# Which pairs of up tiles of an MLP pass take seven quarter products, and a weight split no longer ordered behind evacuations

## The chip, the cores and the metric

The kernel runs on one core of a Trainium2 chip. The metric is the device time of one execution in microseconds (us), as the median of several runs; lower is better. The engines are TensorE (PE; its weight loads are PEld), VectorE (DVE), ScalarE (ACT), GpSimd (POOL) and SyncE (SP, which here only issues DMA transfers). Each engine works through its own instructions strictly in order.

## The reference

Two layers of a decoder trunk in float32, for one sequence of 512 tokens, with D = 1024 and an MLP width of 4096:

```
h = rms_norm(x, ln_mix[l])
x = x + hybrid_mixer(h, ...)        # four token mixers fed by one projection h @ w_in,
                                    # gated sums of their outputs, @ w_out
h = rms_norm(x, ln_mlp[l])
x = x + jnp.square(jax.nn.relu(h @ w_up[l])) @ w_down[l]
```

## The kernel before

**Products.** A float32 product is made of three matmuls, `mm3` (L271): both operands are split into a rounded high part and a rest, and high x high, high x rest and rest x high are added up in PSUM. Weights come from one DRAM array, `wall`, in the order of `plan`. `next_w` (L246) issues a load into one of two `raw` buffers on SP (L255); `split_w` (L258) makes `whi`, a cast on ACT, and then `wlo`, a subtraction on DVE, in one of three buffers each. Nearly all compute instructions are issued through a helper, so that they carry the line L143: tiles are told apart by name.

**Order.** Each engine's order is fixed when the program is built. A scheduler places instructions by priority; `HP()` marks the urgent ones (splits, and the operations that free PSUM). A `NoSync` dependency, as in L264, only tells the scheduler which of two stands first.

**The mixer's first products.** `tok_proj` makes the token-major groups G1, G2 and G3. G2 has 336 columns, four row blocks in four PSUM tiles (`psm`, shown as `tk`). Each is evacuated by two ACT activations, into `sm` and `qe`. `at["hold"]` holds the last of these eight; the next `split_w`, which is that of the first chunk of G3, is ordered behind it. Ahead of that, `rstd` (L348) makes the token scales `rs` on POOL, writes them to DRAM (`rs_dram`, L361) and reads them back across partitions as `rb`, both on POOL's DMA queue. `rsh` is half of `rs`.

**The MLP** (`mlp`, L392) works in four passes of eight up tiles. A pass is four pairs t = 0 to 3, and then a down stage. A normal pair takes two weight chunks of 512 KB through `next_w`, each with 24 matmuls of 512 columns. A pair whose t is in `SEVEN[p]` takes `up_seven` (L420): seven quarter products in place of eight, named A11, S1, S2, S4, S3, A22, A12, of 12 matmuls of 256 columns each. Its four weight quarters (256 KB each, L429) and their sums lie in four `cr` buffers R[0] to R[3]; there are six `cr` buffers in all, and the down stages use them too:

```
B11, S1w, S2w, B22 = R[0][:, lo], R[0][:, up], R[1][:, lo], R[1][:, up]
S3w, all4, B21, B12 = R[2][:, lo], R[2][:, up], R[3][:, lo], R[3][:, up]
sums = {0: ((S1w, B11, B12),), 1: ((S2w, S1w, B22),), 2: ((S3w, B12, B22), (all4, S2w, B21)), 3: ()}
```

The sums are DVE additions (`cr<-cr`), and R[0] to R[3] are split in turn, four splits per pair; R[0] serves A11 and S1, R[1] serves S2 and S4. Before form S3 may add to its PSUM bank, DVE makes U2 = C - U from it (L466, shown as `U<-up,U`). The results are squared in F, cast into `ah` on ACT, and DVE makes the differences `Fs` and the rests `al` (L505 to L511).

The down stage has seven forms too (L639 to L731). Its first is A11, whose PSUM banks (shown as `q`) are those of the fourth pair's tiles, freed by the ReLU that writes F from them (L502). From the second pass on, each result `co` is added into `sum_dram` by an accumulating DMA of POOL's queue (`keep`, L566); so the last of these of one pass run while the up tiles of the next begin. In the last pass `old` (L522) and `xq` (L518) load what the results are joined with.

Of the kernel before, what the change touches and what calls it, by code (L numbers as in the profile page):

```python
# [16 lines left out]
AF = mybir.ActivationFunctionType  # L17
ALU = mybir.AluOpType
# [16 lines left out]
G1K = ((1, 1, 2, 2, 2), (2, 2, 2, 2))  # L35
KORD = ((0, 1, 2, 3, 4, 5, 6, 7), (4, 5, 6, 7, 0, 1, 2, 3))
PASSES = (8, 8, 8, 8)
SEVEN = ((2, 3), (1, 3), (1, 3), (1, 2))
CRB = 6
BIG = 1e30  # L40

# [12 lines left out]
def chunk_plan(l):  # L54
# [30 lines left out]
    for p, nt in enumerate(PASSES):  # L85

        half = nt // 2 * P
        for t in range(0, half, P):
            parts = 2 if t // P in SEVEN[p] else 1
            for i in range(parts):  # L90
# [76 lines left out]
def ins_of(r):  # L167
    return getattr(r, "ins", r)


def trunk(tc, x_in, wall, consts, lps, sgus, out):
    nc = tc.nc
    at = dict(mm=None, side=False, first=None, hold=None)
    V, S, G, T_ = (Paced(tc, e, at) for e in (nc.vector, nc.scalar, nc.gpsimd, nc.tensor))
    HP = lambda off=URGENT: tc.high_priority(offset=off)
    plan = [ch for l in range(NL) for ch in chunk_plan(l)]
    with ExitStack() as es:
# [68 lines left out]
        def next_w(raw=None):  # L246
            kk, n = chunk_shape(plan[pos[0]])
            pos[0] += 1
            L = kk * n
            if raw is None:  # L250
                raw = wpool.tile([P, WCH], F32, name="raw", tag="raw", bufs=WB[0])
            src = wall[off[0]:off[0] + P * L].rearrange("(p l) -> p l", l=L)
            off[0] += P * L
            with HP():
                nc.sync.dma_start(raw[:, :L], src)  # L255
            return split_w(raw, L, n, V.tensor_copy if pos[0] == 1 else S.copy)

        def split_w(raw, L, n, copy=S.copy):  # L258
            hi = wpool.tile([P, WCH], F32R, name="whi", tag="whi", bufs=WB[1])
            lo = wpool.tile([P, WCH], F32R, name="wlo", tag="wlo", bufs=WB[1])  # L260
            with HP():
                c = copy(hi[:, :L], raw[:, :L])
                if at["hold"] is not None:
                    tc.add_manual_dep(ins_of(c), ins_of(at["hold"]).name, V._dep, reason="order")  # L264
                    at["hold"] = None
                r = V.tensor_sub(lo[:, :L], raw[:, :L], hi[:, :L].bitcast(F32))
            at["first"] = r if pos[0] == 1 else None
            return (hi[:, :L].rearrange("p (k n) -> p k n", n=n),
                    lo[:, :L].rearrange("p (k n) -> p k n", n=n))
# [17 lines left out]
        side = []  # L287
# [60 lines left out]
        def rstd(acc, l, late=2):  # L348

            rs, t4 = small["rs"], small["t4"]  # L350
            rb = hpool.tile([P, T], F32, name="rb", tag="rb")

            def gen():
                for _ in range(late):
                    yield
                pa = mmtile("pa", "ms")
                token_sums(pa, acc)
                with HP():
                    V.tensor_scalar(t4, pa[:, 0:4], EPS, None, ALU.add)
                    rpow(rs, t4)  # L360
                G.dma_start(rs_dram[l].rearrange("c p -> p c"), rs)  # L361
                G.dma_start(rb, rs_dram[l].rearrange("c p -> (c p)").partition_broadcast(P))

            side.append(gen())
            return rs, rb
# [26 lines left out]
        def mlp(l, hh, hl, r2, gain, fp, sh, sl):  # L392
# [10 lines left out]
            with tc.tile_pool(name="ap", bufs=1) as ap:  # L403
# [16 lines left out]
                def up_seven(F):  # L420
# [22 lines left out]
                    def form(f, o, i, n, first=True):  # L443
                        if ws[i] is None:
                            for o_, a_, b_ in sums[i]:
                                with HP():
                                    V.tensor_add(o_, a_, b_)
                            ws[i] = split_w(R[i], 512 if i == 3 else 1024, P)
                        w_h, w_l = ws[i]
                        for k in range(4):  # L450
                            bh, bl = moving(f, k)
                            mm3(o, w_h[:, 4 * n + k], w_l[:, 4 * n + k], bh, bl, first and k == 0, k == 3, not first)
                        tick()
# [30 lines left out]
                for p, nt in enumerate(PASSES):  # L484
                    nk = nt // 2
                    ah, al = [], []
                    for t in range(nk):
# [4 lines left out]
                        if t == 1:  # L492
                            early = at["mm"]
                        if t in SEVEN[p]:
                            up_seven(F)
                        for i in range(0 if t in SEVEN[p] else 2):
                            w_h, w_l = next_w()
# [55 lines left out]
                    def use(f, bank, raw, k, first=False):  # L553
                        w_h, w_l = split_w(raw, 1024, 512)
                        for b in range(2):
                            form(f, bank, b, w_h, w_l, k, first)
                        tick()
# [195 lines left out]
        for l in range(NL):  # L753
            with ExitStack() as em:
                x = mixer(tc, em, locals())
            hh, hl = htiles()
            r2 = rstd2(norm(x, lp("ln_mlp"), hh, hl))
            fs = ExitStack()
            fp = fs.enter_context(tc.tile_pool(name="fp", bufs=1))
            forms = quarter_forms(fp, x, lp("ln_mlp"))  # L760
            xs[0].close()
            if l < NL - 1:
                lpt = cpool.tile([P, NLP], F32, name="lp", tag="lp")
                nc.scalar.dma_start(lpt, lps[l + 1])
            nxt, acc = mlp(l, hh, hl, r2, lp("ln_mix"), fp, *forms)
            fs.close()
            if nxt:
                hh, hl = nxt
                rs, rb = rstd(acc, l + 1, 8)
# [3 lines left out]
def mixer(tc, em, env):  # L773
# [9 lines left out]
    def et(name):  # L783
        return yp.tile([P, T], F32, name=name, tag="e", bufs=8)
# [9 lines left out]
    def tt(shape, name, bufs=1, tag=None):  # L794

        p_ = ts if int(np.prod(shape[1:])) % T else tp
        return p_.tile(shape, F32, name=name, tag=tag or name, bufs=bufs)

    if l > 0:
        rs, rb = env["rs"], env["rb"]  # L800
# [14 lines left out]
    def tok_proj(n, kk, chunks, tags, before=None, order=KORD[0], behind=None):  # L815
        pts = {c: mmtile("tk", tags[i]) for i, c in enumerate(chunks)}
        kks = kk if isinstance(kk, tuple) else (kk,) * (KD // kk)
        for k0, kk in zip(np.cumsum((0,) + kks), kks):
            w_h, w_l = next_w(before(k0) if before else None)
            if behind:  # L820
                behind(k0)
            assert not env["at"]["fold"] or order[k0] > 3
            if kk == 1:

                h, first, whole = order[k0], k0 == 0, k0 == KD - 1
                for a, w in ((hh, w_h), (hh, w_l), (hl, w_h)):
                    for c in chunks:
                        env["at"]["mm"] = T_.matmul(pts[c][:, :n], a[h][:, blk(c)], w[:, 0],
                                                    start=first and a is hh and w is w_h, stop=whole and a is hl)
                continue  # L830
            for c in chunks:
                for k in range(kk):
                    mm3(pts[c][:, :n], hh[order[k0 + k]][:, blk(c)], hl[order[k0 + k]][:, blk(c)], w_h[:, k], w_l[:, k],
                        k0 + k == 0, k0 + k == KD - 1)
                if c % 2 == 1:
                    tick()
        return pts
# [49 lines left out]
    else:  # L887
# [28 lines left out]
        rs, rb = rstd(acc[0], 0)  # L916
# [11 lines left out]
    psm = tok_proj(336, 2, range(4), ["mm", "ms", "ms", "ms"])  # L928
    sm = tt([P, 320], "sm").rearrange("p (c w) -> p c w", c=4)
    qe = [et("qe0"), et("qe1")]  # L930
    for c in range(4):
        with HP():
            S.activation(sm[:, c], psm[c][:, 0:80], AF.Identity, scale=rs[:, c:c + 1])
            env["at"]["hold"] = S.activation(qe[c // 2][:, (c % 2) * 256:(c % 2) * 256 + 256], psm[c][:, 80:336],
                                             AF.Identity, scale=rs[:, c:c + 1])
    rsh = tt([P, 4], "rsh")
    V.tensor_scalar(rsh, rs, 0.5, None, ALU.mult)

    def table(n):
        t = et("tab")  # L940
# [403 lines left out]
    for c in range(4):  # L1344
        with HP():
            S.activation(ke[c // 2][:, (c % 2) * 256:(c % 2) * 256 + 256], kvp[c][:, 0:256], AF.Identity,
                         scale=rs[:, c:c + 1])
# [38 lines left out]
    for c in range(4):  # L1386
        with HP():
            S.activation(v2[c // 2][:, (c % 2) * 256:(c % 2) * 256 + 256], pav[c][:, :256], AF.Identity,
                         scale=rs[:, c:c + 1])
    vs = tt([P, 4], "vs")  # L1390
    for c2 in range(2):
        t = et("gv")
        gelu2(v2[c2], t)
        for j in range(2):
            s_ = slice(j * 256, j * 256 + 256)
            c = c2 * 2 + j
# [202 lines left out]
```

## Time and profile before

| | |
|---|---|
| median of 3 runs | 1603.76 us (1603.54 to 1604.75) |
| the profiled execution | 1603.06 us, span of the instructions 1601.3 us |
| PE busy | 1576.8 us, 98% of the span, 8163 matmuls |
| DVE busy | 1238.7 us, 77%, 2127 instructions |
| ACT busy | 756.9 us, 47%, 1168 instructions |
| POOL busy | 144.0 us, 9%, 187 instructions |
| granted TensorE clock | 0.998 over the span |
| DMA | 218.22 MB, mean 136 GB/s |

Busy shares are averages over stages with different limits. The span less PE's busy time, 24.5 us, is all the time in which PE had nothing to run; a stretch in which the granted clock is low counts as busy.

### The profile page before, as it was taken

How to read it: one execution, taken by the hardware profiler on the slowest of the kernel's cores; microseconds unless marked ns; L12 is line 12 of the kernel's file. 1: busy time of each engine (PE TensorE's matmuls, PEld its weight loads, DVE VectorE, ACT ScalarE, POOL GpSimd, SP SyncE). 2: the span in 40 equal slices, each digit the busy share in tenths (PEclk: the TensorE clock that was granted, in tenths of full speed). 3: DMA queues.
4: the chain of work that ended last, by engine and by line, in shares of the span. 5: the costliest groups of instructions: out<-in, count | busy, mean ns of one | idle time of the engine just before them, and what ended most of it. 6: DMA issues, size and time to landing. Idle time of an engine off the chain costs nothing.

```text
span 1601.3 us, 21951 instructions
## 1 busy us (share of the span) xinstructions
PE 1576.8 (98%) x8163; PEld 1322.8 (83%) x8163; DVE 1238.7 (77%) x2127; ACT 756.9 (47%) x1168; POOL 144.0 (9%) x187
## 2 busy tenths in 40 slices
PE   9999999999999999998999999999999999999998
PEld 7888888878888888887888888887888888888887
DVE  6899997645579787867978999975555887867678
ACT  5554224423357474645545433254233674746452
POOL 1322000000001011111013120000000010011110
PEclk9999999999999999999999999999999999999999
DMA  7533322332356466667445232223223465576682
GB/s 179 146 98 110 104 85 99 114 104 95 101 175 165 158 184 158 184 156 221 137 112 155 83 116 96 89 93 135 99 88 111 158 169 176 162 165 171 158 260 83
DMA packets 78411, 218.22 MB, mean 136 GB/s; under 512 B 8896, under 2 KB 16256, under 8 KB 78304
## 3 DMA queue, kind: packets, MB, share of 16 engines
q1 hardware_dynamic: 61360, 175.54, 33.7%
q0 software_dynamic: 16080, 40.27, 13.0%
q8 instruction: 64, 1.05, 0.3%
q10 hardware_dynamic: 864, 1.01, 0.2%
q14 instruction: 43, 0.35, 0.1%
HBM read 192.10 MB, written 21.01 MB: 133 GB/s over the span
## 4 chain that ended last, share of the span: by engine, by line
PE 73%; DVE 13%; issue 5%; ACT 4%; DMA 4%; POOL 0%; SPq 0%; DVEq 0%; ACTq 0%; POOLq 0%
PE g L143 18%; PE up L143 15%; PE tk L143 8%; PE r L143 6%; PE fm L143 6%; PE wo L143 5%; PE q L143 5%; PE p L143 5%; DVE wlo L143 4%; ACT whi L143 2%; DVE sco L143 2%; DMA cr<-in_wall_dram 2%; DMA raw<-in_wall_dram 1%; DVE Fs L143 1%; DVE cr L143 1%
## 5 line engine op out<-in xcount | busy, mean ns | idle before, releaser
L143 ACT CAST whi<-raw 128x1024 fp32r<-128x1024 f32 (+3 forms) x204 | 224.3, 1101 | 199.8 <-DMA raw<-in_wall_dram 64.6
L143 DVE TENSOR_TENSOR wlo<-raw,whi 128x1024 fp32r<-128x1024 f32 (+3 forms) x205 | 262.8, 1283 | 38.5 <-ACT whi L143 37.4
L143 PE MATMUL g<-hh,whi 128*128 128x512 f32 x512 | 200.6, 392 | 0.0
L143 PE MATMUL g<-hh,wlo 128*128 128x512 f32 x512 | 199.5, 390 | 0.0
L143 PE MATMUL g<-hl,whi 128*128 128x512 f32 x512 | 199.3, 389 | 0.0
L143 DVE TENSOR_TENSOR wlo<-cr,whi 128x1024 fp32r<-128x1024 f32 (+1 forms) x144 | 166.6, 1161 | 39.8 <-ACT whi L143 39.5
L143 ACT CAST whi<-cr 128x1024 fp32r<-128x1024 f32 (+1 forms) x144 | 144.3, 1004 | 110.6 <-PE up L143 45.1
L143 PE MATMUL up<-hh,whi 128*128 128x512 f32 (+1 forms) x448 | 155.5, 347 | 0.0
L143 PE MATMUL up<-hh,wlo 128*128 128x512 f32 (+1 forms) x448 | 154.8, 346 | 0.3 <-DVE wlo L143 0.3
L143 PE MATMUL up<-hl,whi 128*128 128x512 f32 (+1 forms) x448 | 154.9, 346 | 0.0
L143 ACT ACTIVATE gs<-gs 128x512 f32<-128x512 f32 x64 | 40.6, 634 | 199.1 <-DVE gs L143 198.9
L143 PEld LDWEIGHTS g<-hh,wlo 128*128 128x128 f32 x512 | 96.1, 188 | 20.3
L143 PEld LDWEIGHTS g<-hh,whi 128*128 128x128 f32 x512 | 96.1, 188 | 19.6
L143 PEld LDWEIGHTS g<-hl,whi 128*128 128x128 f32 x512 | 96.2, 188 | 19.4
L143 PE MATMUL tk<-whi,hh 128*128 128x512 f32 (+2 forms) x304 | 106.9, 358 | 3.9 <-ACT whi L143 3.9
L143 DVE TENSOR_TENSOR cr<-cr 128x512 f32<-128x512 f32 (+1 forms) x80 | 61.7, 793 | 60.4 <-DMA cr<-in_wall_dram 60.1
L143 PE MATMUL tk<-wlo,hh 128*128 128x512 f32 (+2 forms) x304 | 107.3, 355 | 0.2
L143 PE MATMUL tk<-whi,hl 128*128 128x512 f32 (+2 forms) x304 | 106.4, 353 | 0.0
L143 PE MATMUL q<-whi,ah 128*128 128x512 f32 (+1 forms) x260 | 100.9, 392 | 4.2 <-ACT F L143 4.2
L143 DVE TENSOR_TENSOR gs<-g,rb 128x512 f32<-128x512 f32 x64 | 44.1, 689 | 78.7 <-PE g L143 78.6
L143 PE MATMUL q<-whi,al 128*128 128x512 f32 (+1 forms) x260 | 99.8, 389 | 0.0
L143 PE MATMUL q<-wlo,ah 128*128 128x512 f32 (+1 forms) x260 | 99.6, 387 | 0.0
(308 smaller groups left out, 3638.8 us busy)
## 6 DMA issues: line engine op xcount, KB each, us to landing
raw<-in_wall_dram SPq DMA_DIRECT2D x131, 512.0 KB, 4.1
raw<-in_wall_dram SPq DMA_DIRECT2D x64, 640.0 KB, 3.9
cr<-in_wall_dram POOLq DMA_DIRECT2D x48, 512.0 KB, 6.7
cr<-in_wall_dram SPq DMA_DIRECT2D x64, 256.0 KB, 3.4
cr<-in_wall_dram SPq DMA_DIRECT2D x32, 512.0 KB, 3.7
sum_dram<-co POOLq DMA_DIRECT2D x32, 256.0 KB, 6.0
x<-in_x_dram SPq DMA_DIRECT2D x16, 256.0 KB, 4.8
xm_dram<-x SPq DMA_DIRECT2D x16, 256.0 KB, 2.0
```

The lines of the kernel that those rows point to most:

```text
L143: r = f(*a, **k)
```

## The change

Three edits. `SEVEN` moves the first seven-product pair of the second and third pass from t = 1 to t = 2, and leaves the last pass one such pair, t = 2, in place of t = 1 and 2; the weights' order in `wall` follows. In each layer one pair goes from seven quarter products to a normal pair, so that PE has 72 matmuls fewer in all, each of the moved pair twice as wide (84 of 256 columns against 48 of 512). The order of G3's first split behind G2's evacuations goes. `rsh` is made on POOL in place of DVE.

```diff
@@ -35,7 +35,7 @@
 PASSES = (8, 8, 8, 8)
-SEVEN = ((2, 3), (1, 3), (1, 3), (1, 2))
+SEVEN = ((2, 3), (2, 3), (2, 3), (2,))
 CRB = 6
...
@@ -170,7 +170,7 @@
-    at = dict(mm=None, side=False, first=None, hold=None)
+    at = dict(mm=None, side=False, first=None)
...
@@ -259,10 +259,7 @@
             with HP():
-                c = copy(hi[:, :L], raw[:, :L])
-                if at["hold"] is not None:
-                    tc.add_manual_dep(ins_of(c), ins_of(at["hold"]).name, V._dep, reason="order")
-                    at["hold"] = None
+                copy(hi[:, :L], raw[:, :L])
                 r = V.tensor_sub(lo[:, :L], raw[:, :L], hi[:, :L].bitcast(F32))
...
@@ -931,10 +928,10 @@
     for c in range(4):
         with HP():
             S.activation(sm[:, c], psm[c][:, 0:80], AF.Identity, scale=rs[:, c:c + 1])
-            env["at"]["hold"] = S.activation(qe[c // 2][:, (c % 2) * 256:(c % 2) * 256 + 256], psm[c][:, 80:336],
-                                             AF.Identity, scale=rs[:, c:c + 1])
+            S.activation(qe[c // 2][:, (c % 2) * 256:(c % 2) * 256 + 256], psm[c][:, 80:336], AF.Identity,
+                         scale=rs[:, c:c + 1])
     rsh = tt([P, 4], "rsh")
-    V.tensor_scalar(rsh, rs, 0.5, None, ALU.mult)
+    G.tensor_scalar(rsh, rs, 0.5, None, ALU.mult)
```

DVE, layer 0, third pass, where the splits and sums of the pair t = 3 meet those of the pair ahead of it. Before (`raw_5687` and `raw_5720` are the two chunks of the normal pair t = 0; `co` are results of the second pass's down stage; `cr_5764`, `cr_5766` and `cr_5767` are R[0], R[1] and R[2] of the pair t = 1, `cr_5981` to `cr_5984` the four buffers of the pair t = 3; the fourth row is the latter's S2w, which reads its B22):

```order
L143 TENSOR_TENSOR wlo_5690<-raw_5687,whi_5689 128x1024
L143 SCALAR_TENSOR_TENSOR co_5655<-r2_5391,t4_61,Z_5393 128x512
L143 SCALAR_TENSOR_TENSOR co_5656<-r2_5392,t4_61,Z_5393 128x512
L143 TENSOR_TENSOR wlo_5723<-raw_5720,whi_5722 128x1024
L143 TENSOR_TENSOR wlo_5780<-cr_5764,whi_5779 128x1024
L143 TENSOR_TENSOR cr_5983<-cr_5981,cr_5983 128x512
L143 TENSOR_TENSOR wlo_5811<-cr_5766,whi_5810 128x1024
L143 TENSOR_TENSOR cr_5984<-cr_5982,cr_5983 128x512
L143 TENSOR_TENSOR cr_5984<-cr_5983,cr_5982 128x512
L143 TENSOR_TENSOR wlo_5843<-cr_5767,whi_5842 128x1024
```

And of the change (`cr_5841`, `cr_5843` and `cr_5844` are now R[0], R[1] and R[2] of the pair t = 2):

```order
L143 TENSOR_TENSOR wlo_5767<-raw_5764,whi_5766 128x1024
L143 TENSOR_TENSOR wlo_5800<-raw_5797,whi_5799 128x1024
L143 TENSOR_TENSOR wlo_5857<-cr_5841,whi_5856 128x1024
L143 TENSOR_TENSOR Fs_5684<-F_5683 128x512
L143 TENSOR_TENSOR Fs_5684<-F_5683,Fs_5684 128x256
L143 TENSOR_TENSOR al_5686<-F_5683,ah_5685 128x768
L143 TENSOR_TENSOR Fs_5684<-F_5683,Fs_5684 128x256
L143 TENSOR_TENSOR cr_5983<-cr_5981,cr_5983 128x512
L143 TENSOR_TENSOR al_5686<-Fs_5684,ah_5685 128x1024
L143 TENSOR_TENSOR wlo_5888<-cr_5843,whi_5887 128x1024
L143 TENSOR_TENSOR cr_5984<-cr_5982,cr_5983 128x512
L143 TENSOR_TENSOR cr_5984<-cr_5983,cr_5982 128x512
```

The S2w addition of the pair t = 3 stands in both between the first and the second split of the seven-product pair ahead of it. Now two splits of the normal pair t = 1 (`raw_5764`, `raw_5797`) come before that place, and one `al` stands between the addition and the second split.

ACT, layer 0, from G2's last splits (`128x672`) to G3's (`128x1024`), as a difference:

```order
 L143 CAST whi<-raw 128x672 x3
+L143 CAST whi<-raw 128x1024 x2
 L143 ACTIVATE sm<-tk,rs 128x80
 L143 ACTIVATE qe_436<-tk,rs 128x256
...
 L143 ACTIVATE sm<-tk,rs 128x80
 L143 ACTIVATE qe_437<-tk,rs 128x256
-L143 CAST whi<-raw 128x1024 x2
+L143 CAST whi<-raw 128x1024
```

Two casts of G3 have moved from behind the eight evacuations to in front of them.

ACT, layer 0, last pass, where the fourth pair ends and the down stage begins (`raw` are the two chunks of the down stage's A11, `up` the two tiles of the fourth pair, `cr` the first chunk of the down stage's S1). Before:

```order
L143 CAST whi_6881<-raw_6879 128x1024
L143 CAST ah_6634<-Fs_6633 128x1024
L143 ACTIVATE F_6772<-up_6782 128x512
L143 CAST whi_6899<-raw_6897 128x1024
L143 ACTIVATE F_6772<-F_6772 128x512
L143 CAST whi_6921<-cr_6873 128x1024
L143 ACTIVATE F_6772<-up_6815 128x512
```

And of the change:

```order
L143 CAST whi_6818<-raw_6816 128x1024
L143 CAST ah_6571<-Fs_6570 128x1024
L143 CAST whi_6836<-raw_6834 128x1024
L143 ACTIVATE F_6709<-up_6719 128x512
L143 ACTIVATE F_6709<-F_6709 128x512
L143 CAST whi_6858<-cr_6810 128x1024
L143 ACTIVATE F_6709<-up_6752 128x512
```

The first ReLU of the fourth pair, which frees a PSUM bank, has gone behind the cast of A11's second chunk.

## Rows read from the trace of the kernel before

**Rows 1.** The page's first part: busy us, share of the span, instructions.

```profile
PE 1576.8 (98%) x8163; PEld 1322.8 (83%) x8163; DVE 1238.7 (77%) x2127; ACT 756.9 (47%) x1168; POOL 144.0 (9%) x187
```

**Rows 2.** PE by windows, layer 0: us, PE busy, granted clock, DMA share, GB/s.

```profile
486.41:506.81 20.40, 20.40 (x170) 1.00 0.75 202
557.15:567.34 10.19, 10.19 (x86) 1.00 0.51 129
567.34:578.25 10.91, 10.91 (x51) 1.00 0.77 219
578.25:588.32 10.07, 10.07 (x86) 1.00 0.92 231
638.01:649.82 11.81, 10.33 (x86) 1.00 0.46 114
720.49:744.12 23.63, 20.86 (x170) 1.00 0.67 174
```

**Rows 3.** The same of layer 1: third pass t = 1; last pass t = 1, 2.

```profile
1433.00:1447.04 14.04, 11.83 (x86) 0.88 0.51 122
...
1517.70:1542.29 24.59, 22.11 (x169) 0.93 0.70 180
```

**Rows 4.** Timeline of PE: start, us; in brackets the idle before, and its releaser.

```profile
729.40 0.39 PE L143 MATMUL up<-sh,whi 128*128 128x256 f32 x1 [2.77 <-DVE U L143]
...
1441.13 0.38 PE L143 MATMUL up<-sh,whi 128*128 128x256 f32 x1 [2.21 <-DVE U L143]
...
1526.10 0.39 PE L143 MATMUL up<-sh,whi 128*128 128x256 f32 x1 [2.48 <-DVE U L143]
```

**Rows 5.** Timeline of DVE, layer 0: S2w additions of second seven-product pairs, and a split.

```profile
555.37 0.69 DVE L143 TENSOR_TENSOR cr<-cr 128x512 f32<-128x512 f32 x1 [4.36 <-DMA cr<-in_wall_dram]
...
637.85 0.69 DVE L143 TENSOR_TENSOR cr<-cr 128x512 f32<-128x512 f32 x1 [6.81 <-DMA cr<-in_wall_dram]
...
721.85 0.69 DVE L143 TENSOR_TENSOR cr<-cr 128x512 f32<-128x512 f32 x1 [7.75 <-DMA cr<-in_wall_dram]
722.46 1.22 DVE L143 TENSOR_TENSOR wlo<-cr,whi 128x1024 fp32r<-128x1024 f32 x1
```

**Rows 6.** All engines by windows, layer 1, behind the wait at 1441.13.

```profile
1441.80:1445.10 3.30, 3.30 (x18) 3.30 (x17) 2.90 (x5) 0.36 (x1) 1.26 (x2) 0.50 0.89 204
```

**Rows 7.** Timeline of SP: issues of B22 loads, first and third pass, layer 0.

```profile
479.88 0.33 SPq L429 DMA_DIRECT2D cr<-in_wall_dram  x1
...
631.07 0.33 SPq L429 DMA_DIRECT2D cr<-in_wall_dram  x1
```

**Rows 8.** The page's DMA issues: count, KB each, median us to landing.

```profile
cr<-in_wall_dram SPq DMA_DIRECT2D x64, 256.0 KB, 3.4
```

**Rows 9.** Timeline of PE, layer 0: G3's first matmul.

```profile
40.00 1.20 PE L143 MATMUL tk<-whi,hh 128*128 128x512 f32 x4 [1.72 <-ACT whi L143]
```

**Rows 10.** Timelines of DVE, POOL, SP and ACT around G2 and G3, layer 0.

```profile
30.57 0.17 DVE L143 TENSOR_SCALAR rsh<-rs 128x4 f32<-128x4 f32 x1 [1.43 <-POOL rs L143]
...
30.85 0.99 POOL L143 DMA_DIRECT2D rs_dram<-rs  x1 [0.32 <-POOL rs L143]
...
31.95 0.33 SPq L255 DMA_DIRECT2D raw<-in_wall_dram  x1
...
40.44 0.59 POOL L143 DMA_DIRECT2D rb<-rs_dram  x1 [8.59 <-DMA rs_dram<-rs]
...
44.08 1.05 ACT L143 CAST whi<-raw 128x1024 fp32r<-128x1024 f32 x1 [4.13 <-DMA raw<-in_wall_dram]
```

**Rows 11.** Timelines of PE and ACT, layer 0, last pass, start of the down stage.

```profile
756.83 0.50 PE L143 MATMUL q<-whi,ah 128*128 128x512 f32 x1 [1.65 <-ACT F L143]
...
760.16 0.50 PE L143 MATMUL q<-whi,ah 128*128 128x512 f32 x1 [1.44 <-ACT F L143]
...
754.29 1.05 ACT L143 CAST whi<-raw 128x1024 fp32r<-128x1024 f32 x1 [7.42 <-DMA raw<-in_wall_dram]
...
757.10 1.05 ACT L143 CAST whi<-raw 128x1024 fp32r<-128x1024 f32 x1 [0.32 <-DMA raw<-in_wall_dram]
```

## The prediction

> **What bounds the kernel now.** I read the page first, then PE pair by pair in the MLP by windows, then what PE and DVE wait for. PE is busy for 1576.8 of 1603.06 us [rows 1], so little idle time is left to win. But the windows show where it lies. A seven-product pair with no wait takes 10.07 us, a normal pair 10.91, and in the first pass, where the pairs t = 2 and 3 both take seven products, the two follow each other in 20.40 us, all busy [rows 2]. In the later passes the first seven-product pair is longer: 10.19, then 11.81 of which 10.33 busy, then 23.63 of which 20.86 busy for two [rows 2], and in layer 1 14.04 and, for two, 24.59, with granted clocks of 0.88 and 0.93 [rows 3]. So the stretches concerned hold idle time and slow time, and both end with one wait: form S3 waits 2.77, 2.21 and 2.48 us for DVE's U2 [rows 4], and 1.48 us in the third pass of layer 0 by the difference of its window's columns.
>
> **Why U2 is late.** DVE is in order. Ahead of the first pair's second split stands the S2w addition of the *other* seven-product pair, and it sits idle for 4.36, 6.81 and 7.75 us for the load of its B22 [rows 5]. That load goes into the buffer that the first pair's R[0] leaves, so it can be issued only when that is split: at 631.07 in the third pass [rows 7], for an addition that begins at 637.85. Such a load has a median of 3.4 us [rows 8]; here it meets the accumulating writes of the down stage just ended. What comes late is then R[1]'s split, U2, and PE. The start of the addition against the start of the pair orders the cases: 555.37 against 557.15 (1.78 ahead) gives no wait, 637.85 against 638.01 (0.16 ahead) 1.48 us, 721.85 against 720.49 (1.36 behind) 2.77 us [rows 2, 4, 5]. So the wait is the offset plus about 1.5, and it is gone when the addition starts 1.6 us ahead or earlier.
>
> **Second and third pass: t = 1 to t = 2.** The pairs keep their number; where they stand becomes that of the first pass. There B22 is issued at 479.88, 6.53 us ahead of the pair at 486.41 [rows 2, 7], and nothing waits. The new order puts one `al` between the addition and R[1]'s split; at the 1.22 us of a split of that shape [rows 5] the addition has to start 1.6 + 1.2 = 2.8 us ahead of the pair, so the load may take 6.53 - 2.8 = 3.7 us. The addition now comes after a normal pair of 10.91 us more in the pass, when the accumulating writes that lengthened the load have had that much longer to land. I take the first pass's 20.40 us for the two pairs in both passes. Second pass: 20.40 - (10.19 + 10.07) = +0.14 in each layer. Third pass: 20.40 - (11.81 + 10.07) = -1.48 in layer 0, and 20.40 - (14.04 + 10.07) = -3.71 in layer 1 [rows 2, 3]. The bounds of the load are the 3.4 us of the median and the 7.75 of the worst row; it is nearest to the first pass, whose place in the pass it takes, so I take no stall.
>
> **The clock's part.** Behind the wait of 2.21 us in layer 1 the granted clock is 0.50, PE's lower level of 1.2 GHz, for 3.30 us [rows 6], all busy: half of it, 1.65 us, is lost on top. Behind the 2.77 us in layer 0 it is not (1.00 in the window [rows 2]). This is inside the -3.71 and in the last pass's term. By the Trainium skill ("TensorE: Matmul & The Clock Gate", Part 1: The HAM clock gate) the array's default is the half rate, which activity releases; the trace agrees in its 0.50, but one longer wait went without a fall, so no wait can be priced by it with certainty.
>
> **Last pass: one seven-product pair instead of two.** The pair t = 1 becomes normal: PE's own work grows by 10.91 - 10.07 = 0.84 us. With one such pair in the pass, no other pair's addition can stand ahead of its splits. 10.91 + 10.07 = 20.98 in place of 23.63 is -2.65 in layer 0, in place of 24.59 -3.61 in layer 1. The MLP's sum is 2 x 0.14 - 1.48 - 3.71 - 2.65 - 3.61 = -11.17 us.
>
> **The end of the last pass.** There PE already waits 1.65 and 1.44 us for F, since ACT waits for A11's loads: it casts the first chunk at 754.29 after 7.42 us idle, the second at 757.10 [rows 11]. The new order sets the first ReLU behind the second cast. It would start at about 758.1 instead of between the two, some 1.9 us later; the second wait shrinks, since the first group then ends later too, and what remains is one ReLU more on ACT ahead of the second: 0.5 us. In layer 1 I allow up to twice that, together +1.5 us (bounds 0 and the full 2 x 1.9).
>
> **G3's split no longer held.** PE idles 1.72 us ahead of G3 for a cast that the order kept behind the evacuations [rows 9]; with two casts ahead of them this wait goes in both layers, -3.44. In layer 1 one split of 1.22 us then comes between the last additions for the token sums; I take half of it, +0.6. So -2.84 (bounds -3.44 and 0, if evacuations become what is late).
>
> **`rsh` on POOL.** On DVE it costs 0.17 us, and DVE idles 1.43 us for `rs` ahead of it, with the last split of G2 behind it [rows 10]. On POOL it lies inside the 8.59 us in which POOL waits for `rs_dram` before it may issue `rb` [rows 10]: nothing. But the last split of G2 can begin at 30.57 - 1.43 = 29.1 us and be done at 30.0, so that its raw buffer is free for G3's second chunk then: a load issued at 31.95 before [rows 10], now some 0.8 us ahead of the small write issued at 30.85 instead of 1.1 behind.
>
> **The sum.** -11.17 + 1.5 - 2.84 = -12.5; 1603.06 - 12.5 = 1590.6. The runs' median is 0.7 us above the profiled execution, so its time stands for them; I say 1590.5.
>
> **Rivals.**
> 1. *The wait only moves with the pair (slower).* If B22's load takes its 7.75 us in the new place too, U2 is 7.75 - 3.7 = 4.0 us late in four passes (two layers, second and third): +16, 1590.6 + 16 = 1606.6. It decides from a mean of some 6.8 us per load, where 4 x 3.1 = 12.5 is given back. For it: the load still waits for R[0]'s split, and the addition still stands ahead of R[1]'s. Against: the first pass has this order and no wait. Chance 0.07.
> 2. *G3's second chunk stays behind the small write.* That load took from 31.95 to 44.08, 12.1 us [rows 10]. Its cast now stands ahead of the eight evacuations, which would start at 45.1; G3's fourth row block needs a bank that they free, and PE would be there at 40.00 - 1.72 + 18 x 0.227 (10.91 / 48) = 42.4 us. Some 3 us late in layer 0: 1593.7. Against: the load is now issued first. The Trainium skill ("DMA: Bandwidth & Descriptors", Queues, rings and completion order) has each DMA engine alternate between the queues with work, a packet at a time. The 12.1 us agree with a big load sharing its engines with a swarm of small writes, and by that rule being first by 0.8 us would not clear it of them: 1593.7 again. Chance 0.12.
> 3. *One long wait at the last pass's end.* The first wait becomes 1.65 + 1.9 = 3.5 us in one piece, longer than those that slowed the clock. With 1.65 us lost to that in both layers: 1593.9. For it: the 2.21 us of layer 1; against: the 2.77 of layer 0. Chance 0.13.
> 4. *The gain is given back.* A load or an evacuation elsewhere is late by what PE gains, above all in the last pass, where DMA is what ACT waits for: 1600 to 1603, no change that counts. Chance 0.06.
>
> **How the numbers follow.** The forecast has the remaining chance, 0.62, with a range of its own of 1587 to 1594. Rivals 2 and 3 end inside 1593 to 1596 even with the other bounds of their terms; the lower end adds the bound of no loss at the pass's end and in G3, and a little less elsewhere: 1585. To 1600 no more than rivals 1 and 4 are left out with a part of the forecast's own spread. A measurement of this kernel can tell 0.2%, 3.2 us: faster holds the forecast, rivals 2 and 3: 0.87, less a little for a mishap not named: 0.85. Same 0.07, slower 0.08.
>
> **What would show it.** Right: 72 matmuls fewer; the pairs t = 2 and 3 of the second and third pass in 20.4 us without a wait for U; no stretch at 0.50 in layer 1's MLP; the last pass's t = 1, 2 in 21.0; no idle PE ahead of G3; DVE's S2w additions without a wait of over 4 us. Wrong: a wait for U2 in the new place of the pair, a cast of G3's second chunk that starts at 44 us in front of the evacuations, or a granted clock of 0.50 behind the start of the last down stage.

## The result, and the profile after

The changed kernel takes 1584.03 us (median of 4 runs, 1583.81 to 1584.15), the kernel before in the same runs 1603.65 (1601.48 to 1604.75): ratio 0.9879, 95% interval 0.9862 to 0.9896, so 19.6 us or 1.2% faster. In another set of runs it took 1584.47 against 1603.23 (0.9884, 0.9870 to 0.9898). The forecast was 1590.5 with a range of 1585 to 1600: the direction was right, the gain half as large again as forecast, and the time 1 us under the range.

The page's first part, as in [rows 1]:

```profile
PE 1573.6 (99%) x8091; PEld 1318.2 (83%) x8091; DVE 1226.1 (77%) x2103; ACT 753.9 (48%) x1160; POOL 144.9 (9%) x189
```

The 72 matmuls are gone, and the span of 1582.3 us leaves PE 8.7 us idle, where it was 24.5. PE by windows (us, PE busy, granted clock, DMA share, GB/s), to be held against [rows 2, 3]: the pairs t = 2 and 3 of the second and the third pass of layer 0; the last pass of layer 0 from t = 1 to t = 3, and behind it the stretch of the down stage's first two forms, A11 and S1, which both write `q` (called the A11 stage from here on); the third pass's t = 2 and 3, the last pass's t = 2 and the A11 stage of layer 1:

```profile
566.44:586.80 20.36, 20.36 (x169) 1.00 0.78 202
647.37:667.74 20.37, 20.37 (x170) 1.00 0.76 202
717.40:728.30 10.90, 10.90 (x49) 1.00 0.85 251
728.30:738.38 10.08, 10.08 (x86) 1.00 0.97 280
738.38:749.28 10.90, 10.90 (x50) 1.00 0.97 311
749.28:760.92 11.64, 11.49 (x49) 1.00 0.68 219
1433.50:1453.87 20.37, 20.37 (x170) 1.00 0.79 200
1514.44:1524.51 10.07, 10.07 (x86) 1.00 1.04 289
1535.42:1546.95 11.53, 11.47 (x49) 1.00 0.61 212
```

Every pair shown takes its 10.07 to 10.08 or 10.90 us, or 20.36 to 20.37 for two, all busy, at a granted clock of 1.00; no wait for U is left. What the forecast did not have is the end of the last pass: the matmul that waited 1.65 us for F [rows 11] starts at 749.28 without a wait. ACT there, after:

```profile
745.78 1.05 ACT L143 CAST whi<-raw 128x1024 fp32r<-128x1024 f32 x1 [4.66 <-DMA raw<-in_wall_dram]
746.74 1.05 ACT L143 CAST ah<-Fs 128x1024 fp32r<-128x1024 f32 x1
747.69 1.05 ACT L143 CAST whi<-raw 128x1024 fp32r<-128x1024 f32 x1
748.65 0.58 ACT L143 ACTIVATE F<-up 128x512 f32<-128x512 f32 x1
```

The ReLU does stand behind the second cast, as the order said, but that cast no longer waits for its load, and the first one waits 4.66 us where it waited 7.42. Counted from the first matmul of the pass (709.61 before, 706.54 after), that first load of A11 is there after 44.7 us before [rows 11] and after 39.2 us now. The loads into `cr` for the down stage begin earlier in the pass too, 11.5 us into it in place of 16.6; SP's issue of the first one, before and after:

```profile
726.17 0.33 SPq L543 DMA_DIRECT2D cr<-in_wall_dram  x1
718.03 0.42 SPq L540 DMA_DIRECT2D cr<-in_wall_dram  x1
```

Before, the DMA engines were little used in the pair t = 1, where the changed kernel has a share of 0.85 (the third window above):

```profile
720.49:730.56 10.07, 7.30 (x58) 1.00 0.27 70
```

The stages, each from its first matmul to that of the next in the timelines of PE, before and after (us); the forecast's own terms beside them:

| stage | layer 0 | layer 1 | sum | forecast |
|---|---|---|---|---|
| G2 and G3, up to the transposes of the index keys | 32.85 to 30.49 | 33.16 to 30.84 | -4.7 | -2.8 |
| rest of the mixer, up to the output projection | 364.79 to 366.30 | 365.45 to 365.88 | +1.9 | 0 |
| second pass, up tiles | 42.69 to 42.12 | 41.94 to 42.13 | -0.4 | +0.3 |
| third pass, up tiles | 43.67 to 42.13 | 45.90 to 42.13 | -5.3 | -5.2 |
| last pass, up tiles and A11 stage | 60.12 to 54.38 | 58.92 to 54.27 | -10.4 | -6.3 + 1.5 |
| sum | | | -18.9 | -12.5 |

So of the 6.4 us between them, 5.6 lie in the last pass. The rest of the mixer is 1.9 us longer in this pair of traces; whether that is the change's doing stays open (last section).

### The profile page after: what moved, and what is told of

Read it like the earlier page. It is cut to its first block, busy times and chain, and to the rows that moved or that the text cites. A ratio compares the mean times of both kernels' runs of the same rounds, so it can differ in the third digit from the quotient of the medians.

```text
span 1582.3 us, 21761 instructions
## 1 busy us (share of the span) xinstructions
PE 1573.6 (99%) x8091; PEld 1318.2 (83%) x8091; DVE 1226.1 (77%) x2103; ACT 753.9 (48%) x1160; POOL 144.9 (9%) x189
## 4 chain that ended last, share of the span: by engine, by line
PE 71%; DVE 16%; issue 5%; ACT 5%; DMA 2%; POOL 1%; SPq 0%; DVEq 0%; POOLq 0%; ACTq 0%
PE g L143 18%; PE up L143 15%; PE r L143 8%; PE tk L143 7%; PE q L143 6%; PE fm L143 5%; PE p L143 4%; PE wo L143 4%; DVE wlo L143 4%; DVE sco L143 2%; ACT whi L143 2%; DMA raw<-in_wall_dram 1%; DVE Fs L143 1%; DVE m L143 1%; ACT F L143 1%
## 5 line engine op out<-in xcount | busy, mean ns | idle before, releaser
L143 ACT CAST whi<-raw 128x1024 fp32r<-128x1024 f32 (+3 forms) x208 | 228.5, 1100 | 220.6 <-DMA raw<-in_wall_dram 81.7
L143 DVE TENSOR_TENSOR wlo<-raw,whi 128x1024 fp32r<-128x1024 f32 (+3 forms) x209 | 267.6, 1281 | 77.5 <-ACT whi L143 65.2
L143 DVE TENSOR_TENSOR wlo<-cr,whi 128x1024 fp32r<-128x1024 f32 (+1 forms) x136 | 157.8, 1165 | 45.7 <-ACT whi L143 45.4
L143 ACT CAST whi<-cr 128x1024 fp32r<-128x1024 f32 (+1 forms) x136 | 136.9, 1008 | 105.4 <-PE up L143 40.4
L143 PE MATMUL up<-hh,whi 128*128 128x512 f32 (+1 forms) x456 | 160.4, 352 | 0.0
L143 PE MATMUL up<-hl,whi 128*128 128x512 f32 (+1 forms) x456 | 159.6, 350 | 0.0
L143 PE MATMUL up<-hh,wlo 128*128 128x512 f32 (+1 forms) x456 | 159.6, 350 | 0.0
L143 PEld LDWEIGHTS up<-hh,whi 128*128 128x128 f32 x456 | 86.2, 189 | 12.6 <-ACT F L143 1.0
```

Source lines behind the costliest of these rows:

```text
L143: r = f(*a, **k)
```

## The experiments

**The table alone, and the mixer's edits alone.** In the kernel before:

```diff
-SEVEN = ((2, 3), (1, 3), (1, 3), (1, 2))
+SEVEN = ((2, 3), (2, 3), (2, 3), (2,))
```

> The kernel before with the new table of seven-product pairs alone; the order of G3's split behind the evacuations and rsh on VectorE stay. If the parts add up, all that the MLP's windows gained comes: in the traces of before and after the third pass differs by -1.5 and -3.8 us (layers 0 and 1), the last pass with the down stage's A11 by -5.7 and -4.7, the second by -0.6 and +0.2, -16.1 in all: 1587.3 us, PE idle 1.72 us ahead of G3 in both layers as before. Rival: the MLP's loads needed the earlier start that the mixer's edit gave; then the waits at the start of the last down stage (3.1 us in layer 0, 1.1 in layer 1) are back, 1591 us.

Measured: 1588.34 us (4 runs) against 1601.89, ratio 0.9912 (0.9897 to 0.9927): -13.6. In its trace the third pass takes 42.13 and 42.14 us, the last pass's up tiles 42.74 in both layers and the A11 stage 11.14 and 11.12, no longer than in the changed kernel: the waits that the rival expected are not there, and the MLP needs nothing of the mixer's edit. (The trace is of the shortest execution, 1585.15 us.) And the reverse, the changed kernel with the old table:

```diff
-SEVEN = ((2, 3), (2, 3), (2, 3), (2,))
+SEVEN = ((2, 3), (1, 3), (1, 3), (1, 2))
```

> The changed kernel with the old table: only the order and rsh differ from before. By the two traces G3 starts 1.9 and 1.7 us earlier and is through 2.4 and 2.2 us earlier, and the mixer gives back 1.4 in layer 0 and 0.4 in layer 1: 1600.5 us, with the MLP as before (waits for U of 1.5, 2.8, 2.2 and 2.5 us). Rival, that what is given back in layer 0 is an accident of one execution: 1599.0 us.

Measured: 1596.56 against 1601.89, ratio 0.9965 (0.9952 to 0.9978): -5.3, more than either number expected. G2 and G3 take 30.49 and 30.84 us, as in the changed kernel, and the rest of the mixer is 1.5 and 0.3 longer than in the trace of before. The remainder lies in waits that this edit does not touch: the third pass of layer 1 takes 43.71 us here and 45.90 in the trace of before, where the clock fell behind the wait for U, and the last pass of layer 0 with its A11 stage 57.74 here and 60.12 there. Such waits change from one execution to the next (the kernel before runs from 1597.55 to 1605.65 in one set of 17, the changed one from 1583.81 to 1584.88 in all 8). The two parts add up: -13.6 - 5.3 = -18.9.

**Last pass alone, middle passes alone.** In the kernel before, one of these in place of the old table:

```diff
+SEVEN = ((2, 3), (1, 3), (1, 3), (2,))
...
+SEVEN = ((2, 3), (2, 3), (2, 3), (1, 2))
```

> The kernel before with one seven-product pair in the last pass (t = 2) and the other passes as before. Theory of the buffers: with four cr buffers fewer in use there, the down stage's loads go out earlier and A11's two loads land in time; the last pass and A11 gain 5.7 us in layer 0 and 4.7 in layer 1: 1592.8 us, with waits of under 0.3 us for F at the start of the last down stage. Rival theory, that those waits went because PE's and the loads' times had shifted against each other in the passes before: only -2.7 and -3.6 come, the waits for F stay at 1 us and more, 1596.9 us.

> The kernel before with the pair moved from t = 1 to t = 2 in the second and third pass, and the last pass as before. Both theories: the third pass gains 1.5 and 3.8 us, the second 0.4 in sum, 1597.6 us. Theory of the buffers: the waits for F at the start of the last down stage stay (1.7 and 1.4 us in layer 0, 1.1 in layer 1). Rival theory of the shift: they shrink to under 0.3 us, and the time is 1593.5 us.

Measured: the last pass alone 1594.12 against 1601.89, 0.9951 (0.9935 to 0.9968), -7.8; the middle passes alone 1597.03, 0.9971 (0.9959 to 0.9982), -4.9. The traces tell the theories apart without the spread of the totals. With the last pass alone it takes, with the A11 stage, 53.88 us in both layers, together 107.8; with the old table in that pass the two layers take 119.0 (before), 117.0 (the mixer's edits alone) and 116.4 (the middle passes alone). The two A11 stages with the last pass alone, by windows of PE:

```profile
753.53:764.67 11.14, 11.14 (x50) 1.00 0.64 220
1546.23:1557.37 11.14, 11.14 (x50) 1.00 0.63 223
```

With the middle passes alone the waits for F stand as before (PE, layers 0 and 1):

```profile
756.46 0.50 PE L143 MATMUL q<-whi,ah 128*128 128x512 f32 x1 [1.32 <-ACT F L143]
...
1548.54 0.50 PE L143 MATMUL q<-whi,ah 128*128 128x512 f32 x1 [1.46 <-ACT F L143]
```

Whether the last pass has one or two seven-product pairs decides over the wait at its end; the shift of PE by what the passes ahead gain does not remove it. The middle passes bring their forecast: 42.14 us in the third pass of both layers.

**U without its wait, the pairs where they were.** In the kernel before, the additions for forms S2, S4, S3 and A22 of a seven-product pair are ordered behind the U2 of the one ahead:

```diff
+                    prev = at.get("u2")
...
-                                    V.tensor_add(o_, a_, b_)
+                                    r = V.tensor_add(o_, a_, b_)
+                                if i in (1, 2) and prev is not None:
+                                    tc.add_manual_dep(ins_of(r), ins_of(prev).name, V._dep, reason="order")
...
-                        V.tensor_sub(U2, C, U)
+                        at["u2"] = V.tensor_sub(U2, C, U)
```

> The kernel before with its old table of pairs; only the additions S2w, S3w and all4 of a seven-product pair are ordered on VectorE behind the U2 of the seven-product pair ahead of it. Theory of the order: VectorE stood idle for B22's load in front of the splits that U2 needs; now the waits for U (1.5, 2.8, 2.2, 2.5 us in the trace of before) go although no pair is moved and the load stays as slow, with what the clock took: -9 to -12 us against the kernel before in the same runs, the waits for F at the last down stages as before. Rival, that the place of the pair in the pass, where DMA is crowded, is what makes it late: the second pair's own splits are late in their turn, and less than 4 us come.

Measured: 1605.97 against 1603.85, ratio 1.0016 (1.0004 to 1.0028): 2 us more in place of 9 to 12 less. The rival's "less than 4 us" fits the time, but not for its reason. No wait for U is left in the trace, with no pair moved, so it was the order on DVE that held U2 up; the third pass takes 41.93 us in both layers (43.67 and 45.90 before), 5.7 less. But in the last pass the time comes back as a wait for F, in layer 1 with 3 us on top. PE in layers 0 and 1, and ACT ahead of the first of the two waits:

```profile
757.75 0.80 PE L143 MATMUL q<-whi,ah 128*128 128x512 f32 x1 [4.59 <-ACT F L143]
...
1555.07 0.80 PE L143 MATMUL q<-whi,ah 128*128 128x512 f32 x1 [5.94 <-ACT F L143]
...
754.27 1.04 ACT L143 CAST whi<-raw 128x1024 fp32r<-128x1024 f32 x1 [9.37 <-DMA raw<-in_wall_dram]
```

Its up tiles take 46.91 and 48.27 us, with the old 47.22 and 46.41; with the A11 stage 59.9 and 61.9, with the old 60.1 and 58.9. A11's first load is there 43.4 and 44.8 us into the pass, where it was there after 44.7 and 43.9: with the old table the last pass was bound by A11's loads, not by U. (Of the rest, 3.5 us are lost in the first pass, where the new order sets `al` late: its down stage takes 40.48 and 40.68 us instead of 38.82. Some 2.6 us lie in the mixer, which the edit does not touch.) All engines by windows show the DMA share (next to last column) in layer 0's last pass, here from the first seven-product pair on:

```profile
721.70:731.90 10.20, 10.20 (x86) 10.18 (x85) 9.09 (x15) 7.53 (x11) 0.56 (x1) 1.00 0.41 114
731.90:742.00 10.10, 10.10 (x85) 9.93 (x84) 9.93 (x17) 7.83 (x13) 4.09 (x5) 1.00 0.78 188
742.00:747.00 5.00, 5.00 (x25) 4.16 (x24) 3.41 (x5) 2.83 (x5) 0.00 (x0) 1.00 1.05 261
747.00:757.70 10.70, 6.16 (x28) 4.76 (x26) 2.35 (x3) 3.43 (x4) 0.00 (x0) 0.88 1.03 343
```

Ten microseconds at 0.41, ten at 0.78, and then 16 at the full rate with PE waiting in them. This run and the changed kernel also issue A11's first load at the same place in the pass, 30.4 and 30.3 us into it (here, then in the changed kernel):

```profile
741.25 0.33 SPq L546 DMA_DIRECT2D raw<-in_wall_dram  x1
736.88 0.38 SPq L540 DMA_DIRECT2D raw<-in_wall_dram  x1
```

Its cast starts 13.0 us behind the issue here and 8.9 us behind it in the changed kernel. So the load is not issued earlier there; more of the others are through. By their landing in the traces, five loads into `cr` are still under way at that moment here, and two there.

**Without the accumulating writes.**

```diff
                             if p == 0:
                                 nc.sync.dma_start(dst, tiles[b])
-                            else:
-                                nc.gpsimd.dma_start(dst, tiles[b], accum_op=ALU.add)
```

> The kernel before without the accumulating writes of the second and third pass into sum_dram (these two passes' share of the MLP's result is left out). Theory: these writes make B22's load slow in the third and the last pass; without them it takes 3 to 4 us in place of 6.8 and 7.7, the S2w addition starts 3 us earlier, and the waits for U in the third and last pass go below 0.3 us: 8 to 12 us less. Rival, that the load is slow because of the other weight loads on the same queue: waits for U of 1.5 us and more stay.

One run: 1589.39 us, 14 less than before, where 8 to 12 were expected, and no wait for U at all. DVE's S2w addition in layer 0's third pass, which waited 6.81 us [rows 5]:

```profile
632.77 0.69 DVE L143 TENSOR_TENSOR cr<-cr 128x512 f32<-128x512 f32 x1 [2.88 <-DMA cr<-in_wall_dram]
```

The load was issued at 629.92 and is there 2.85 us later. So the writes made it slow. The waits for F stay (2.34 and 1.44 us in layer 0): they are another cause's. With the A11 stage the last pass takes 57.5 and 55.1 us in place of 60.1 and 58.9, so without these writes a part of what U's waits cost there is not lost again.

**The down stage's loads late again.** In the changed kernel:

```diff
-                        if t == 1:
+                        if t == (3 if p == last else 1):
                             early = at["mm"]
```

> The changed kernel with the last pass's cr loads of the down stage marked to go behind the third pair (t = 2) in place of the first, so that they are issued about where two seven-product pairs let them out before. Theory of the buffers: they meet A11's two loads again, ScalarE waits for these, and the waits for F at the start of the last down stage are back, 1 to 2 us in each layer: 2 to 4 us more than the changed kernel. Rival, that the early issue of the cr loads has nothing to do with it: the same time within 0.5 us.

Measured: 1594.72 against 1603.85, ratio 0.9944 (0.9923 to 0.9965), where the changed kernel has 0.988: some 10 us of its gain lost, in two stages; the A11 stage takes 16.15 and 16.21 us instead of 11.64 and 11.53. The size is beyond what was expected and the place is another: A11's first load is now there early (cast at 741.90), and it is the first `cr` chunk that is late. ACT and PE, layer 0:

```profile
753.13 1.04 ACT L143 CAST whi<-cr 128x1024 fp32r<-128x1024 f32 x1 [5.40 <-DMA cr<-in_wall_dram]
```

```profile
756.25 0.80 PE L143 MATMUL q<-whi,ah 128*128 128x512 f32 x1 [3.54 <-ACT ah L143]
```

ACT is in order: the second ReLU of the fourth pair and its `ah` stand behind that cast. So the expected meeting with A11's two loads is not what costs here: what is not moved in the first half of the pass is late at its end, whichever load is last. The size is no measure of what the change gains, though. SP issues the first `cr` load at 736.95 here, 30.5 us into the pass, and two seven-product pairs let it out 16.6 us into it: the edit holds these loads back by much more than the old table did.

**`rsh` back on DVE.** In the changed kernel:

```diff
-    G.tensor_scalar(rsh, rs, 0.5, None, ALU.mult)
+    V.tensor_scalar(rsh, rs, 0.5, None, ALU.mult)
```

> The changed kernel with rsh on VectorE as before. Theory of the queue: G2's last split waits for rs again, G3's second load is issued some 1 us behind the small write of rs instead of ahead of it and lands at 44 us; its cast stands ahead of the evacuations, and layer 0 loses 3 us at G3's fourth row block: 3 us more than the changed kernel. Rival: the load lands by 36 us anyway, and nothing changes (within 0.5 us).

Measured: 1590.13 against 1603.85, ratio 0.9915 (0.9896 to 0.9933), beside 0.988: about 5 us lost. The theory of the queue holds, with a higher price: its trace is 5.4 us longer than that of the changed kernel, and the stage alone 7.5, of which 5.01 are the wait below and the rest falls behind it, at a granted clock of 0.50. ACT and PE, layer 0:

```profile
43.28 1.04 ACT L143 CAST whi<-raw 128x1024 fp32r<-128x1024 f32 x1 [11.70 <-DMA raw<-in_wall_dram]
```

```profile
45.55 0.47 PE L143 MATMUL qiT<-cst,qr 128*128 128x128 f32 x1 [5.01 <-ACT qe L143]
```

The load was issued at 31.48, 1.1 us behind the small write at 30.39, and G3 takes 22.62 us instead of 15.09 up to the index keys' transposes. In the changed kernel the same load goes out at 29.86 and the write at 31.06; its cast starts at 34.54, and waits for PE, not for the load:

```profile
34.54 1.05 ACT L143 CAST whi<-raw 128x1024 fp32r<-128x1024 f32 x1 [2.60 <-PE tk L143]
...
43.69 1.05 ACT L143 CAST whi<-raw 128x1024 fp32r<-128x1024 f32 x1 [4.80 <-DMA raw<-in_wall_dram]
```

The second row is the next chunk, issued at 33.22: now this one takes 10.5 us, but its cast stands behind the evacuations, and PE needs it only at 44.31.

**Further than the change.** Beside a second run of the changed kernel, two tables more, and both together:

> The changed kernel once more, beside the next three, so that they are compared with it on one chip: 1584 us, about 18 us less than the kernel before.

```diff
+SEVEN = ((2, 3), (2, 3), (2, 3), (1,))
...
+SEVEN = ((1, 2, 3), (2, 3), (2, 3), (2,))
...
+SEVEN = ((1, 2, 3), (2, 3), (2, 3), (1,))
```

> The changed kernel with the last pass's one seven-product pair at t = 1 in place of t = 2. Theory of the buffers: its cr buffers, and the tiles that the loads of old and xm go into, come free a pair earlier; the transfers are spread over more of the pass, and the 0.5 us that A11 still loses in each layer (11.64 and 11.53 against 11.09 in the second pass) goes: 1 us less than the changed kernel. Rival: the pair now starts 11 us after the down stage ahead of it, beside its accumulating writes, its own quarters land late, and 1 to 4 us more.

> The changed kernel with three seven-product pairs in the first pass (t = 1, 2, 3). No accumulating write runs there: each B22 has a pair's time to land, and 10.91 - 10.07 = 0.84 us come in each layer, 1.7 us less than the changed kernel. Rival: waits for U of 0.4 to 0.8 us, which single executions showed in the first pass, come at two places instead of one and in both layers, and eat it: no change within 0.5 us, or up to 2 us more.

> Both together: 2.7 us less than the changed kernel if both theories hold and add up; if only one does, what that one alone brings.

Measured, against 1603.23: the changed kernel 1584.47; the last pass's pair at t = 1 1592.23 (0.9931, 0.9918 to 0.9944); three pairs in the first pass 1595.55 (0.9953, 0.9939 to 0.9967); both 1602.13 (0.9998, 0.9987 to 1.0010). Neither theory won. With t = 1 the A11 stage does fall to 11.12 us in both layers, but the up tiles take 46.53 and 46.92 instead of 42.74: the down stage's transfers now go ahead of the last normal pairs' own loads, and these are late (in layer 0 one issued at 726.36 is cast at 739.05). With three pairs in the first pass it takes 47.57 and 47.98 us instead of 42.98 and 42.93, and in layer 1 its A11 stage takes 15.54 instead of 11.09, behind a wait of 2.36 us for `al`. PE, layer 1, one kernel each:

```profile
1530.00 0.50 PE L143 MATMUL up<-hh,whi 128*128 128x512 f32 x1 [1.60 <-ACT whi L143]
```

```profile
1291.04 0.38 PE L143 MATMUL up<-hh,whi 128*128 128x256 f32 x1 [1.41 <-ACT whi L143]
```

The waits with three pairs are for splits and for `al`, not for U: neither the theory nor its rival had named them. The losses add up: 7.8 and 11.1 us against the changed kernel one by one, 17.7 together. The changed kernel is the fastest that was tried.

## Why the prediction was right and wrong

- **The late U2, and the passes in which its pair moves: right** in mechanism and place. That DVE's order held U2 up is shown by undoing the order alone, that the accumulating writes made the load slow by leaving them out. The size, -5.3 for -5.2 in the third pass, is in part luck: the term was read from the same trace of before against which the change is held. In the other traces with the old table the two layers' third passes take 43.78 and 43.71 us (the mixer's edits alone) and 45.43 and 47.04 (the last pass alone), which would make it -3.2 and -8.2. The second pass moved 0.7 us more than the term, at a wait for `wlo` in its first pair that the term had left out.
- **The last pass: the step that failed**, in "The end of the last pass": "The new order sets the first ReLU behind the second cast ... together +1.5 us". It came to a gain of about 4: the stage gained 10.4 where -6.3 was forecast for its pairs. The step kept the landing of A11's loads fixed against PE, and read only what the new order does to ACT. With the table's edit that pass needs four `cr` buffers fewer, and the down stage's loads go out from 718.03 on, 5 us earlier in the pass, into time that had been nearly idle (DMA share 0.85 in the pair t = 1, where it was 0.27). A11's first load is then there 39.2 and 37.2 us into the pass, and not 43 to 45. One or two pairs in that pass decide over the wait, and holding the `cr` loads back far enough brings it back. What SP and POOL issue earlier was no part of the step.
- Where the landing does stay, the step's mechanism shows: in the run of the order alone ACT's first ReLU stands behind both casts of A11 too (the second cast starts at 756.17, the ReLU at 757.11), and PE waits 4.59 us in one piece.
- **The last pass's -2.65 and -3.61** were met, but not for the reason given: in the run of the order alone, with two pairs and no wait for U, the last pass gains nothing, since its loads bind. Had the change only taken U's wait away there, this term would have been wrong by its whole size, by that run.
- **G3: right in kind, too small,** and outside its bounds of -3.44 and 0. G3 starts 1.90 and 1.85 us earlier after G2's first matmul, and is 0.46 and 0.47 us shorter up to the index keys' transposes; the 0.6 allowed in layer 1 did not come. That makes -4.7 for -2.8. The rest of the mixer, for which nothing was forecast, is 1.9 us longer in this pair of traces; that this belongs to the change is not shown (last section).
- **Rival 2, the second chunk behind the small write**, did not happen, but its mechanism is real and its price higher than its 3 us: 5 us of the changed kernel's gain hang on `rsh`, the edit that the sum costed at nothing. The Trainium skill ("DMA: Bandwidth & Descriptors", Queues, rings and completion order) has each DMA engine alternate between the queues that have work, and the rival drew from it that being first by 0.8 us would not clear the load. It did, by 1.2 us. This is no test of the rule: the small write, issued at 31.06, has no packet on POOL's queue before 32.7, when 0.46 MB of the load issued at 29.86 have moved.
- **Rivals 1 and 3** did not come: no load kept U2 waiting in the new place, and no wait at the end of the last pass is left that could slow the clock. In the run of the order alone rival 3's one long wait is there, 4.59 and 5.94 us, and the granted clock behind it is 0.50. **Rival 4** was wrong on the last pass; on the mixer it is open.

## What to carry to other kernels

Before a wait is priced as a gain, ask what ends it if it goes: here the last pass's loads stood right behind, and the same time came back under another name. An edit that uses fewer buffers also lets later loads out earlier; look for them in the queues of the DMA issuers, and in the DMA share of the stretch just ahead. And an operation of 0.17 us on an in-order engine can be worth 5 us, if a large load's issue hangs on it and a write in many small pieces is about to start.

## What was not expected of the hardware

- The crowding behind the write of `rs` (128x4 values, 2 KB, some 9 us from issue to landing in layer 0) is not that of one load but of the time. The loads of 512 KB shown here that were issued 1.1 to 2.2 us behind it were cast 10.5 to 12.1 us after their issue (the median to landing is 4.1 in the page of before), and one issued 1.2 us ahead was not held up. The DMA engines look busy meanwhile, and move little: a share of 1.11 for 31 GB/s (changed kernel, by windows of PE):

```profile
33.40:40.00 6.60, 6.60 (x41) 1.00 1.11 31
```

- A wait of PE in the mixer comes and goes from one execution to the next. In the changed kernel DVE waits 2.74 us for MB, which is read back from DRAM (1.30 in the trace of before), and then index selection on DVE is late and PE waits for it, where it did not before. But the same wait stands in traces with the old mixer, as with the order alone, where DVE's wait is 2.66. PE in layer 0, the changed kernel and that one:

```profile
258.39 0.38 PE L143 MATMUL lg<-kS,qS 128*128 128x256 f32 x1 [1.05 <-DVE yl L143]
...
260.86 0.39 PE L143 MATMUL lg<-kS,qS 128*128 128x256 f32 x1 [1.06 <-DVE yl L143]
```

  From the index keys' transposes up to the output projection a layer takes 364.8 to 366.5 us in the six traces with the old mixer and 365.7 to 367.4 in the seven with the new one. So some of what G3 gained may be lost again there, but one pair of traces cannot show it, and why that transfer sometimes takes longer was not tried.
- Behind PE's waits of 3.38 and 3.54 us (the late loads), 4.59 and 5.94 us (the order alone) and 5.01 us (`rsh` on DVE) the granted clock was 0.50, so that the time lost is more than the wait. Behind shorter ones the length does not tell: it was 0.50 behind 1.46 us (the middle passes alone, layer 1) and 2.21 us [rows 4, 6], and 1.00 behind 2.76 us (the mixer's edits alone, layer 1) and the 2.77 us of [rows 4].
